# SyncE's loads in written order through the mixing of a diffusion trunk, with shared decay buffers and later closings

## The chip, the cores and the metric

The kernel runs on one core of one Trainium2 chip. Its time is the device time of one execution in microseconds; the median over three executions is given. The core's engines are TensorE (PE, with its weight loads as PEld), VectorE (DVE), ScalarE (ACT), GpSimd (POOL) and SyncE (SP). SyncE computes nothing: its queue issues nearly all loads and many stores. Each engine works through its own queue in order, and waits on semaphores for the others.

## The reference

One layer of a diffusion trunk over 1024 latent tokens and 256 context tokens, width 1024, in float32. It has a half-step SwiGLU feed-forward, then the mixing, then a second half-step feed-forward, each modulated by a condition vector. The mixing projects the normalised tokens by one matrix into four retention heads (key and value width 128) and four gated linear attention heads, called GLA below (key width 64, value width 128, with a low-rank gate). Cut to its core:

```python
x = x + 0.5 * m_l[2] * swiglu(modulate(rms_norm(x, norm1_w), m_l[0], m_l[1]), ffn1_w1, ffn1_w3, ffn1_w2)
...  # the same for ctx; then, on both normalised and modulated:
p_lat, p_ctx = jnp.split(h_lat @ w_in, IN_SPLITS, axis=-1), jnp.split(h_ctx @ w_in, IN_SPLITS, axis=-1)

# retention, one step of the scan over chunks of 128 tokens
scores = jnp.einsum('bhid,bhjd->bhij', qc, kc) * decay
o = jnp.einsum('bhij,bhje->bhie', scores, vc) + jnp.einsum('bhid,bhde->bhie', qc * q_dec, s)
s = chunk_dec * s + jnp.einsum('bhjd,bhje->bhde', kc * k_dec, vc)

# GLA, one step of the scan over chunks of 64 tokens, g the log gates
b = jnp.cumsum(gc, axis=-2)
rel = jnp.exp(jnp.where(tri[:, :, None], b[:, :, :, None, :] - b[:, :, None, :, :], -jnp.inf))
scores = jnp.einsum('bhid,bhjd,bhijd->bhij', qc, kc, rel)
o = jnp.einsum('bhij,bhje->bhie', scores, vc) + jnp.einsum('bhid,bhde->bhie', qc * jnp.exp(b), s)
s = jnp.exp(b_last[:, :, 0, :])[..., None] * s + jnp.einsum('bhjd,bhje->bhde', kc * jnp.exp(b_last - b), vc)

# closing
r = merge_heads((o_ret - mu) * lax.rsqrt(var + EPS)) * ret_norm_w * jax.nn.silu(p[3])
gl = merge_heads(o_gla * lax.rsqrt(mean(o_gla * o_gla) + EPS)) * gla_norm_w * jax.nn.silu(p[7])
y = jnp.concatenate([r, gl], axis=-1) @ w_out
x = x + m_l[5] * y
x = x + 0.5 * m_l[8] * swiglu(modulate(rms_norm(x, norm3_w), m_l[6], m_l[7]), ffn2_w1, ffn2_w3, ffn2_w2)
return rms_norm(x, final_norm_w)
```

Both scans run in both directions. The scans over the latent tokens start from the final states of the scans over the context. Every head's output is normalised over its 128 channels (GLA by the root mean square, retention by mean and variance), multiplied by a weight and a gate, and projected back by `w_out`.

## The kernel before

A product in float32 is made of three matmuls with the operands split into a high and a low part (`whi`, `wlo` of the weights, `hh`, `hl` of the activations): ScalarE copies the high part (line 62), VectorE subtracts it (line 63). A weight goes through a ring of six `raw` buffers, loaded by SyncE (line 273), and is then split. Activations lie as 128 channels by 512 tokens, in two halves of the latent tokens, `tg` 0 and 1; context tokens are 256 columns wide, and for the value projections a weight tile is 288 wide, 256 values and 32 gate columns.

The program runs in phases: the first feed-forward, the context's projections (`ctx_proj`, whose results go to memory as `cgk`, `crk`, `cgv`, `crv`, line 1112 for the last), the mixing's set-up (`mix_setup`: position tables, `wg`, `p89Tc`), the mixing itself (`lat_phase`), the output projection (`mixed_in` and `mixed_out`), the second feed-forward.

In `lat_phase` a small planner writes the program. Its filling is the list of large projections of the latent tokens (`lat_units`; a unit such as `gv0` is one projection of a few heads). Beside it run four lanes, written as generators: the context's final states, the gates, the four GLA heads and the four retention heads. The planner holds a clock of TensorE's time (`self.now`) and guesses of when VectorE, ScalarE and GpSimd come free (`self.clk`, moved by `self.w`). A lane yields the time at which its next step has its operands; the planner emits that step once its time has come, and otherwise the next piece of a projection.

TensorE takes the instructions in the order in which they were written (`pe_order`). On the other engines a scheduler with priorities sets the order: it may put a load or a copy far ahead of its place in the program. Weight loads have a raised priority (line 300 and what calls it).

A head's output of one half ends in a chain that is called its closing. GLA: square the output and sum it, take the power −1/2 on GpSimd (`pow_half`, line 1168), scale by it on ScalarE (line 1375, tile `t`). Retention: statistics (lines 1489 and 1491), power on GpSimd, scale on VectorE (line 1500, tile `t2r`). Then `finish`: four transposes on TensorE (line 1150), a multiply by the norm's weight, and by the gate where its tile is ready (such a block is "gated"), and a store to `mixd` in memory. `mixed_in` loads the blocks back (line 1672), multiplies by the gate those that lack it, and splits them.

`decays` makes three decay tables per retention head by exponentials on ScalarE (line 1200), combines them on VectorE and stores them to `decd`. The GLA heads build their within-chunk products in levels: tiles `AB` (lines 1262, 1276) are scaled on VectorE, copied to `zq` and `zk` (lines 1265 to 1267), and multiplied on TensorE (lines 1285 and 1320).

Of the kernel before, what the change touches and what calls it, by code (L numbers as in the profile page):

```python
# [10 lines left out]
F32 = mybir.dt.float32  # L11
# [5 lines left out]
P = 128  # L17
# [13 lines left out]
class Trunk:  # L31
# [834 lines left out]

    def pe_order(self):
        return self.tc.manual_schedule(engines={mybir.EngineType.PE})

# [276 lines left out]
    def finish(self, on, tg, wcol, hb, pool):  # L1146
        nc = self.nc
        pt = self.psB()
        for c in range(4):
            nc.tensor.transpose(pt[:, c * P:(c + 1) * P], on[:, c * P:(c + 1) * P], self.ident)  # L1150
        mx = self.t2(pool)
        if hb in self.gated:
            sg = self.tile(pool, [P, 512], F32, "sg", 2)
            nc.sync.dma_start(sg, self.sgd[hb * P:(hb + 1) * P, tg * 512:(tg + 1) * 512])
            nc.vector.scalar_tensor_tensor(out=mx, in0=pt, scalar=wcol, in1=sg, op0=ALU.mult, op1=ALU.mult)
            self.w("v", 0.75)
        else:
            self.late.add((hb, tg))
            nc.scalar.activation(mx, pt, AF.Copy, scale=wcol)
            self.w("a", 0.62)  # L1160
        self.w("p", 0.6)
        self.store.dma_start(self.mixd[hb * P:(hb + 1) * P, tg * 512:(tg + 1) * 512], mx)
# [7 lines left out]
    def gate_lane(self, pool):  # L1170
# [18 lines left out]
        for h in range(4):  # L1189
            yield max(self.clk["a"], self.now + 5 * (h > 0)), 0, ()  # L1190
            self.decays(h, pool)
            self.done[f"D{h}"] = self.w("p", 0.6, self.w("v", 0.6, self.w("a", 1.6)))

    def decays(self, h, pool):
        nc = self.nc
        tab = lambda i: self.tab[:, i * P:(i + 1) * P]
        dec, u = self.tile(pool, [P, 3, P], F32, "dec", 1), self.t2(pool)[:, :P]
        lf, lb = self.lg[:, h:h + 1], self.lg[:, 4 + h:5 + h]
# [4 lines left out]
        nc.vector.tensor_tensor(out=dec[:, 0, :], in0=dec[:, 0, :], in1=u, op=ALU.add)  # L1203
        self.store.dma_start(self.decd[h], dec.rearrange("p i t -> p (i t)"))

# [26 lines left out]
    def gla_lane(self, h, pool):  # L1232
# [126 lines left out]
        for tg in LATTG:  # L1359
# [10 lines left out]
            r = self.tile(pool, [P, 4], F32, "rr", 4)  # L1370
            self.pow_half(r, ss, 1.0 / P)
            on = self.t2(pool)
            for c in range(4):
                s = slice(c * P, (c + 1) * P)
                nc.scalar.activation(on[:, s], po[:, s], AF.Copy, scale=r[:, c:c + 1])
            t = self.w("v", 0.2, self.w("v", 0.7, self.w("a", 0.62)))
            ons.append((self.w("a", 1.15, self.w("p", 1.3, t)), on))
        for tg in LATTG:
            yield ons[tg][0], 0.9, ()
            self.finish(ons[tg][1], tg, self.col("gla_norm_w")[:, h:h + 1], 4 + h, pool)  # L1380

    def ret_lane(self, h, pool):
# [95 lines left out]
        for tg in LATTG:  # L1478
# [14 lines left out]
            self.pow_half(r, mv[:, :, 1], 1.0)  # L1493
            t = self.w("p", 1.3, self.w("v", 1.4))
            if tg == 0:
                ready, sc, qf = decay(1, ps)
            on = t2()
            for c in range(4):
                s = slice(c * P, (c + 1) * P)
                nc.vector.tensor_scalar(out=on[:, s], in0=po[:, s], scalar1=mv[:, c, 0:1], scalar2=r[:, c:c + 1],  # L1500
                                        op0=ALU.subtract, op1=ALU.mult)
            ons.append((self.w("v", 1.5, t), on))
        for tg in LATTG:
            yield ons[tg][0], 0.9, ()
            self.finish(ons[tg][1], tg, self.col("ret_norm_w")[:, h:h + 1], h, pool)
# [120 lines left out]
    def lat_phase(self, pool):  # L1626
# [17 lines left out]
        lanes = [[g, 0, 0, ()] for g in lanes]  # L1644
        with self.pe_order():
            for lane in list(lanes):
# [107 lines left out]
    def run(self):  # L1754
# [243 lines left out]
        def feed2():  # L1998
# [42 lines left out]
UNITS = ("gv0", "gk0", "gq0", "rk0", "rq0", "rv0", "rk1", "rq1", "gk1", "gq1", "gv1", "gg0", "rk2", "rq2", "rv1", "rg0", "gg1",  # L2041
         "rk3", "rq3", "rg1", "gg2", "rg2", "gg3", "rg3")
LAG = 0.7
WAHEAD, WLIVE = 3, 5
# [98 lines left out]
```

## Time and profile before

| | us |
|---|---|
| runs | 2121.08, 2123.88, 2125.47 |
| median | 2123.88 |
| the profiled execution's own time | 2122.97 |
| its span, first to last instruction | 2121.1 |
| TensorE busy | 2097.8 |
| VectorE, ScalarE, GpSimd busy | 1522.5, 961.3, 176.9 |
| last matmul of the context's projections starts | 913.14 |
| first matmul of the mixing's projections starts | 913.26 |

In a timeline row stand: start, duration, engine, line, operation, output <- inputs, shapes, count; in brackets the engine's idle time before it and what ended it. A row of waits names the waiting instruction, what released it, the total, the count and the longest. In a row of windows stand: the stretch and its length; the busy time of TensorE, its weight loads, VectorE, ScalarE and GpSimd, each with its number of instructions; the granted TensorE clock as a share of full speed; the share of the DMA engines; GB/s. A queue is marked by a q (SPq is SyncE's).

### The profile page before, as it was taken

How to read it: one execution, taken by the hardware profiler on the slowest of the kernel's cores; microseconds unless marked ns; L12 is line 12 of the kernel's file. 1: busy time of each engine (PE TensorE's matmuls, PEld its weight loads, DVE VectorE, ACT ScalarE, POOL GpSimd, SP SyncE). 2: the span in 40 equal slices, each digit the busy share in tenths (PEclk: the TensorE clock that was granted, in tenths of full speed). 3: DMA queues.
4: the chain of work that ended last, by engine and by line, in shares of the span. 5: the costliest groups of instructions: out<-in, count | busy, mean ns of one | idle time of the engine just before them, and what ended most of it. 6: DMA issues, size and time to landing. Idle time of an engine off the chain costs nothing.

```text
span 2121.1 us, 32909 instructions
## 1 busy us (share of the span) xinstructions
PE 2097.8 (99%) x11558; PEld 1807.9 (85%) x11558; DVE 1522.5 (72%) x2810; ACT 961.3 (45%) x1786; POOL 176.9 (8%) x294
## 2 busy tenths in 40 slices
PE   8999999999999999999999999999999999999998
PEld 7888888888889999987889988888888888888888
DVE  7889999766677765857675565567866676666676
ACT  4433434345545555667442443344433434344552
POOL 0101111110000000011010000100011110111000
PEclk9999999999999999999999999999999999999999
DMA  9266867569886654476462445452244443466773
GB/s 339 85 219 234 281 218 257 185 203 338 277 290 206 205 180 159 142 239 224 140 194 95 162 141 178 158 208 75 90 140 154 158 167 136 148 243 234 237 241 124
DMA packets 214726, 408.50 MB, mean 193 GB/s; under 512 B 26208, under 2 KB 52256, under 8 KB 214560
## 3 DMA queue, kind: packets, MB, share of 16 engines
q1 hardware_dynamic: 185456, 330.24, 47.5%
q0 software_dynamic: 18848, 61.87, 7.3%
q10 hardware_dynamic: 10256, 14.29, 1.8%
q8 instruction: 90, 1.47, 0.3%
q14 instruction: 76, 0.62, 0.1%
HBM read 320.04 MB, written 86.26 MB: 192 GB/s over the span
## 4 chain that ended last, share of the span: by engine, by line
PE 47%; issue 3%; DVE 1%; POOL 1%; ACT 0%; POOLq 0%; DVEq 0%; ACTq 0%
PE psa L67 9%; PE psa L69 8%; PE psa L68 8%; PE psb L69 5%; PE psb L68 5%; PE psb L67 5%; PE psa L1574 3%; PE psb L1285 1%; PE psb L1441 1%; POOL rr L1168 0%; PE psb L1485 0%; PE psb L1459 0%; PE psb L1349 0%; PE psb L1150 0%; PE psb L1365 0%
## 5 line engine op out<-in xcount | busy, mean ns | idle before, releaser
L62 ACT ACTIVATE whi<-raw 128x512 fp32r<-128x512 f32 (+1 forms) x471 | 292.7, 624 | 564.0 <-PE psa L68 182.5
L67 PE MATMUL psa<-hh,whi 128*128 128x512 f32 (+1 forms) x1444 | 531.8, 368 | 0.2 <-ACT s L332 0.2
L69 PE MATMUL psa<-hh,wlo 128*128 128x512 f32 (+1 forms) x1444 | 525.7, 364 | 0.0
L68 PE MATMUL psa<-hl,whi 128*128 128x512 f32 (+1 forms) x1444 | 525.6, 364 | 0.0
L63 DVE TENSOR_TENSOR wlo<-raw,whi 128x512 fp32r<-128x512 f32 (+1 forms) x471 | 318.5, 679 | 226.2 <-ACT whi L62 222.6
L67 PEld LDWEIGHTS psa<-hh,whi 128*128 128x128 f32 x1444 | 273.2, 189 | 47.0 <-issue 5.3
L69 PEld LDWEIGHTS psa<-hh,wlo 128*128 128x128 f32 x1444 | 272.8, 189 | 43.4
L68 PEld LDWEIGHTS psa<-hl,whi 128*128 128x128 f32 x1444 | 273.1, 189 | 40.8 <-DVE hl L63 0.3
L67 PE MATMUL psb<-hh,whi 128*128 128x512 f32 (+1 forms) x680 | 259.6, 382 | 0.0
L69 PE MATMUL psb<-hh,wlo 128*128 128x512 f32 (+1 forms) x680 | 259.4, 382 | 0.0
L68 PE MATMUL psb<-hl,whi 128*128 128x512 f32 (+1 forms) x680 | 259.4, 382 | 0.0
L68 PEld LDWEIGHTS psb<-hl,whi 128*128 128x128 f32 x680 | 127.8, 188 | 24.8
L69 PEld LDWEIGHTS psb<-hh,wlo 128*128 128x128 f32 x680 | 127.8, 188 | 24.7
L67 PEld LDWEIGHTS psb<-hh,whi 128*128 128x128 f32 x680 | 127.8, 188 | 24.6
L285 ACT ACTIVATE whi<-s 128x512 fp32r<-128x512 f32 (+1 forms) x164 | 101.0, 620 | 87.0 <-PE psa L68 38.0
L290 DVE TENSOR_TENSOR wlo<-s,whi 128x512 fp32r<-128x512 f32 (+1 forms) x164 | 106.9, 675 | 29.6 <-ACT whi L285 29.4
L373 POOL DMA_DIRECT2D gd<-s x154 | 83.7, 543 | 370.5 <-DVE s L364 285.1
L130 DVE CUSTOM_DVE_ANT_0 junk<-ada,condc,cols 128x1024 bf16<-128x1024 f32 x62 | 79.2, 1278 | 5.9 <-DMA ada<-in_adaT 3.8
L1168 POOL TENSOR_TENSOR nr<-nr,mhalf 128x4 f32<-128x4 f32 (+1 forms) x11 | 10.9, 992 | 687.3 <-DVE nr L1167 445.5
L372 DVE TENSOR_TENSOR s<-s,s 128x512 f32<-128x512 f32 x88 | 59.0, 684 | 0.5
L359 ACT ACTIVATE s<-s 128x512 f32<-128x512 f32 x57 | 36.0, 632 | 47.8 <-DVE s L336 47.7
L1574 PE MATMUL psa<-whi,hh 128*128 128x256 f32 x192 | 56.1, 292 | 0.0
(428 smaller groups left out, 3941.4 us busy)
## 6 DMA issues: line engine op xcount, KB each, us to landing
raw<-in_w SPq DMA_DIRECT2D x242, 256.0 KB, 3.4
s<-in_w SPq DMA_DIRECT2D x198, 256.0 KB, 4.1
gd<-s POOLq DMA_DIRECT2D x154, 256.0 KB, 2.9
ada<-in_adaT SPq DMA_DIRECT2D x76, 512.0 KB, 4.6
hh<-gd SPq DMA_DIRECT2D x58, 256.0 KB, 4.1
hl<-gd SPq DMA_DIRECT2D x58, 256.0 KB, 4.1
sd<-s POOLq DMA_DIRECT2D x44, 256.0 KB, 3.1
raw<-sd SPq DMA_DIRECT2D x44, 256.0 KB, 2.8
```

Source lines behind the costliest of these rows:

```text
L62: nc.scalar.activation(hi, src, AF.Copy)
L63: (eng or nc.vector).tensor_tensor(out=lo, in0=src, in1=hi.bitcast(F32), op=ALU.subtract)
L67: mm(ps, wa[0], xa[0], start=start, stop=False, skip_group_check=more)
L68: mm(ps, wa[0], xa[1], start=False, stop=False, skip_group_check=more)
L69: mm(ps, wa[1], xa[0], start=False, stop=stop, skip_group_check=more)
L130: nc.vector.tensor_tensor_reduce(out=self.junk, in0=t, in1=self.cs[s], scale=1.0, scalar=self.col("ada_b")[:, j:j + 1], op0=ALU.mult, op1= ...
L285: self.nc.scalar.activation(hi[:, :n], src, AF.Copy)
L290: self.nc.vector.tensor_tensor(out=lo, in0=src, in1=hi.bitcast(F32), op=ALU.subtract)
L359: self.nc.scalar.activation(o, t, AF.Silu)
L372: sub = lambda o, a, b: nc.vector.tensor_tensor(out=o, in0=a, in1=b, op=ALU.subtract)
L373: put = lambda i, t: self.store.dma_start(self.gd[i, f // 2], t)
L1574: mm(o, x[p], y[q], start=k == 0 and n == 0 and c % 2 == 0, stop=k == KD - 1 and n == 2, skip_group_check=True)
```

## The change

The diff, whole but for two lines that set a constant's place:

```diff
-    def pe_order(self):
-        return self.tc.manual_schedule(engines={mybir.EngineType.PE})
+    def pe_order(self, *more):
+        return self.tc.manual_schedule(engines={mybir.EngineType.PE, *more})
@@ finish
         if hb in self.gated:
-            sg = self.tile(pool, [P, 512], F32, "sg", 2)
+            sg = self.t2(pool)
             nc.sync.dma_start(sg, self.sgd[hb * P:(hb + 1) * P, tg * 512:(tg + 1) * 512])
@@ gate_lane
         for h in range(4):
-            yield max(self.clk["a"], self.now + 5 * (h > 0)), 0, ()
+            yield max(self.clk["a"], self.now + DECAT * (h > 0)), 0, ()
             self.decays(h, pool)
@@ decays
-        dec, u = self.tile(pool, [P, 3, P], F32, "dec", 1), self.t2(pool)[:, :P]
+        t, u = self.t2(pool)[:, :3 * P], self.t2(pool)[:, :P]
+        dec = t.rearrange("p (i t) -> p i t", i=3)
...
-        self.store.dma_start(self.decd[h], dec.rearrange("p i t -> p (i t)"))
+        self.store.dma_start(self.decd[h], t)
@@ gla_lane
             self.pow_half(r, ss, 1.0 / P)
+            yield self.w("p", 1.3, self.w("v", 0.9, self.w("a", 0.62))), 0, ()
             on = self.t2(pool)
             for c in range(4):
                 s = slice(c * P, (c + 1) * P)
                 nc.scalar.activation(on[:, s], po[:, s], AF.Copy, scale=r[:, c:c + 1])
-            t = self.w("v", 0.2, self.w("v", 0.7, self.w("a", 0.62)))
-            ons.append((self.w("a", 1.15, self.w("p", 1.3, t)), on))
+            ons.append((self.w("a", 1.15), on))
         for tg in LATTG:
-            yield ons[tg][0], 0.9, ()
+            yield ons[tg][0] + FIN, 0.9, ()
@@ ret_lane
-            t = self.w("p", 1.3, self.w("v", 1.4))
+            t = self.w("p", 1.3, self.w("v", 1.45))
             if tg == 0:
                 ready, sc, qf = decay(1, ps)
+            yield t, 0, ()
             on = t2()
...
-            ons.append((self.w("v", 1.5, t), on))
+            ons.append((self.w("v", 1.4), on))
         for tg in LATTG:
-            yield ons[tg][0], 0.9, ()
+            yield ons[tg][0] + FIN, 0.9, ()
@@ lat_phase
-        with self.pe_order():
+        with self.pe_order(mybir.EngineType.SP):
@@ constants
+DECAT = 12
+FIN = 2
```

It has four parts. Inside the mixing SyncE's queue, too, keeps the order in which the planner writes it. The decay tables lie in the ring of six shared `t2` buffers in place of a single buffer of their own, and the heads' tables are 12 us apart in the plan where they were 5 apart; the gate tiles of `finish` lie in the same ring. In the closings the scaling becomes a step of its own, which the planner emits at the time at which it expects GpSimd's power. The closing transposes stand 2 us later in the plan.

The instructions stay nearly the same: 10748 on TensorE in both, 2812 on VectorE (two multiplies of `mixed_in` become two in `finish`), two copies fewer on ScalarE, 1293 on SyncE. From the mixing on a line number of the profile is one or two higher in the changed kernel (1276 becomes 1277, 1500 becomes 1502).

The rows below are those of the engines' queues. First SyncE's queue before the change, in the middle of the context's projections (`raw` is a weight's buffer, `in_wgv0` the first projection of the mixing, `in_w12` a weight of the feed-forward):

```order
L273 DMA raw_1994_9066<-in_w12 128x512
L273 DMA raw_2173_9817<-in_wgv0 128x288
L273 DMA raw_2180_9827<-in_wgv0 128x288
L273 DMA raw_2183_9833<-in_wgv0 128x288
L273 DMA raw_2186_9839<-in_wgv0 128x288
L273 DMA raw_2189_9857<-in_wgv0 128x288
L273 DMA raw_2192_9875<-in_wgv0 128x288
L1091 DMA cgk<-s_2028_9169 128x256
```

The same weight, `raw_2173`, in SyncE's queue of the changed kernel, 57 places further on, at the start of the mixing:

```order
L1112 DMA crv<-s_2145_9744 128x256
L929 DMA wg_2150_9762<-in_wgb 16x4x64
L928 DMA wg_2150_9762<-in_wgf 16x4x64
L929 DMA wg_2150_9762<-in_wgb 16x4x64
L932 DMA p89Tc_2151_9768<-p89d 32x256
L939 DMA t2_2152_9774<-in_lvlmask 128x128
L939 DMA t2_2154_9778<-in_lvlmask 128x128
L939 DMA t2_2156_9782<-in_lvlmask 128x128
L939 DMA t2_2158_9786<-in_lvlmask 128x128
L1021 DMA t2_2170_9812<-crk 128x256
L1022 DMA t2_2171_9813<-crv 128x2x128
L273 DMA raw_2173_9817<-in_wgv0 128x288
```

The first weight loads of the mixing moved from ahead of the context's stores to behind the last of them, the tables, the masks and two loads of the context's results. On TensorE nothing moved here: the first matmul on the high part of this weight follows the last matmul of the context's projections in both. On ScalarE the table load and the exponential `kd` (line 915) stand ahead of the copy of line 1111 that this `crv` store saves; before, they stood behind it.

Second, VectorE's queue in the second GLA and retention heads, before (`bst` and `bmv` are a retention closing's statistics, `rr` what GpSimd raises to its power, `AB0` and `AB1` the GLA head's tiles):

```order
L1489 BN_STATS bst_2629_12359<-psb_2628_12346 128x6 x4
L1491 BN_AGGR bmv_2630_12360<-bst_2629_12359 128x2 x4
L1167 TENSOR_SCALAR rr_2631_12369<-bmv_2630_12360 128x4
L1276 TENSOR_TENSOR AB0_2537_11781<-AB0_2537_11781,L_2536_11778 128x2x8x32
L1500 TENSOR_SCALAR t2r_2632_12372<-psb_2628_12346,bmv_2630_12360,rr_2631_12369 128x128 x4
L1276 TENSOR_TENSOR AB1_2540_11790<-AB1_2540_11790,L_2539_11787 128x2x8x32
```

and in the changed kernel:

```order
L1490 BN_STATS bst_2632_12413<-psb_2631_12400 128x6 x4
L1492 BN_AGGR bmv_2633_12414<-bst_2632_12413 128x2 x4
L1167 TENSOR_SCALAR rr_2634_12423<-bmv_2633_12414 128x4
L1277 TENSOR_TENSOR AB0_2565_11891<-AB0_2565_11891,L_2564_11888 128x2x8x32
L1277 TENSOR_TENSOR AB1_2568_11900<-AB1_2568_11900,L_2567_11897 128x2x8x32
L1502 TENSOR_SCALAR t2r_2636_12486<-psb_2631_12400,bmv_2633_12414,rr_2634_12423 128x128 x4
```

The scaling of the retention output moved behind the second `AB`.

Third, TensorE's queue at the last closing but one, near the end of the mixing, in the changed kernel (`psa` with `hh0`, `hl0` are the last projections, `t2_2966` is GLA's scaled output):

```order
L69 MATMUL psa_2972_14630<-hh05_2007_9096,wlo_2957_14527 128x512
L1150 MATMUL psb_2974_14654<-ident_4_82,t2_2966_14600 128x128 x4
L67 MATMUL psa_2972_14630<-hh06_2009_9098,whi_2956_14526 128x512
```

This closing, of the last GLA head and the first half, stands 30 matmuls of projections ahead of the output projection; the last one of all, for the second half, stands 12 ahead of it. Before, the last closing was a retention head's, with 90 matmuls of projections behind it. That GLA head's two closings are gated in the changed kernel and were not before.

## The prediction

> **What bounds the kernel now.** I read the page's busy table and the core's clock first, then TensorE's waits in the stretch that the change touches, then for each of them what its releaser had waited for, and last SyncE's timeline where the stretch begins.
>
> ```profile
> PE 2097.8 (99%) x11558; PEld 1807.9 (85%) x11558; DVE 1522.5 (72%) x2810; ACT 961.3 (45%) x1786; POOL 176.9 (8%) x294
> core 0: 2121.1 us, clock 0.995
> ```
>
> TensorE is busy for 99% of the span, at nearly its full clock. The change neither adds nor removes a matmul (10748 instructions stand on TensorE in both). So there are only three ways to move the time: TensorE's idle time, its clock, and the order in which matmuls of different shapes follow each other. The first question is how much idle time the mixing has to give.
>
> ```profile
> PE psb L1285 <- DVE zk L1266: 1.8, 1, 1.8
> PE psb L1150 <- DVE t2r L1500: 1.6, 1, 1.6
> PE psb L1320 <- DVE AB L1276: 1.2, 1, 1.2
> PE psb L1459 <- ACT t L1159: 0.8, 1, 0.8
> PE psb L1441 <- DVE Sr L1448: 0.4, 1, 0.4
> ```
>
> These are all of TensorE's waits from 930 to 1420 us, by line and releaser (us in total, times, the longest): 1.8 + 1.6 + 1.2 + 0.8 + 0.4 = 5.8 us. The first one costs more than its idle time. The windows behind it show the granted clock (PEclk, the third figure from the end):
>
> ```profile
> 1012.00:1013.00 1.00, 0.54 (x5) 0.57 (x5) 1.00 (x4) 0.13 (x1) 0.00 (x0) 0.98 0.77 240
> 1013.00:1014.00 1.00, 1.00 (x7) 1.00 (x6) 1.00 (x4) 0.00 (x0) 0.04 (x1) 0.50 0.09 35
> 1016.00:1017.00 1.00, 1.00 (x9) 1.00 (x9) 1.00 (x3) 0.95 (x4) 0.00 (x0) 0.82 0.00 0
> ```
>
> After 1.8 us of idling the clock stood at half from about 1013.0 to 1016.4. That is 3.4 us in which half the work was lost, 1.7 us. So at most 5.8 + 1.7 = 7.5 us can be won in the mixing.
>
> **The waits that the change goes after.** Each has its cause one step further back:
>
> ```profile
> ACT dec L1200 <- DMA decd<-dec: 2.1, 1, 2.1
> DVE t2r L1500 <- POOL rr L1168: 1.0, 1, 1.0
> 1142.83 1.36 DVE L1500 TENSOR_SCALAR t2r<-psb,bmv,rr 128x128 f32<-128x128 f32 x4 [0.93 <-POOL rr L1168]
> 1144.11 1.28 DVE L1276 TENSOR_TENSOR AB<-AB,L 128x512 f32<-128x512 f32 x2
> ```
>
> The single `dec` buffer held ScalarE for 2.1 us until its store had read it; `zk` stands behind it, and TensorE's 1.8 us behind that. With the table in one of six shared buffers and the heads 12 us apart this wait has no cause left. In the second and third stall VectorE stood in front of GpSimd's power: 1.0 and 0.93 us. At 1142.83 VectorE idled 0.93 and scaled for 1.36 before the `AB` that TensorE missed by 1.2. In the changed order that `AB` stands ahead of the scaling, as the rows in the section on the change show, so VectorE comes to it 0.93 + 1.36 = 2.3 us earlier, more than 1.2. In the second and the fourth stall the late work is the scaling or the copy of a closing itself; there the closing is put 2 us later in the written order. The edit removes no work: two multiplies move on VectorE and two copies leave ScalarE, both with idle time in the mixing, and they are worth nothing to TensorE. What is late next is unknown: the lanes now run in another order from their second head on, so small stalls of the same kind can fall elsewhere. Bounds: 0, and the 5.8 us that the old order had. I take 2, about two of the smaller ones. Gain: (5.8 − 2) + 1.7 = 5.5 us.
>
> Matmuls of 128 columns between those of 512 have a price too:
>
> ```profile
> 1357.83 0.39 PE L69 MATMUL psa<-hh,wlo 128*128 128x512 f32 x1
> 1358.06 0.60 PE L1150 MATMUL psb<-ident,t2r 128*128 128x128 f32 x4
> 1358.41 0.48 PE L67 MATMUL psa<-hh,whi 128*128 128x512 f32 x1
> 1358.73 0.39 PE L68 MATMUL psa<-hl,whi 128*128 128x512 f32 x1
> ```
>
> The first matmul after a switch takes 0.32 to the next start, the one before the transposes 0.23, so a switch costs about 0.09. I count 80 switches back to large matmuls in the mixing before and 84 after: +0.4 us.
>
> **The queue of loads.** This term decides. Before, the scheduler moved the first six weight loads of the mixing some 50 us ahead; in the change SyncE's queue keeps the written order, and the first weight stands behind everything that was written before it. What stands there has these issue times before (SyncE's timeline; weight loads that stood between them are left out):
>
> ```profile
> 861.46 0.33 SPq L273 DMA_DIRECT2D raw<-in_wgv  x1
> ...
> 914.18 0.38 SPq L1112 DMA_DIRECT2D crv<-s  x1
> ...
> 915.66 0.39 SPq L1112 DMA_DIRECT2D crv<-s  x1
> 916.14 0.70 SPq L928 DMA_DIRECT2D wg<-in_wgf  x1
> ...
> 918.90 0.58 SPq L928 DMA_DIRECT2D wg<-in_wgf  x1
> 919.53 0.59 SPq L929 DMA_DIRECT2D wg<-in_wgb  x1
> 920.17 0.58 SPq L932 DMA_DIRECT2D p89Tc<-p89d  x1
> 920.80 1.36 SPq L939 DMA_DIRECT2D t<-in_lvlmask  x3
> ...
> 923.16 0.42 SPq L1021 DMA_DIRECT2D t<-crk  x1
> 923.63 0.43 SPq L1022 DMA_DIRECT2D t<-crv  x1
> ```
>
> The last `crv` store is the gate: it saves what ScalarE copies out of the last context matmul, so it can't be issued before that copy. In ScalarE's changed order a table load and one small exponential stand ahead of it.
>
> ```profile
> 913.14 0.28 PE L69 MATMUL psa<-whi,hl 128*128 128x256 f32 x1
> 913.26 0.30 PE L67 MATMUL psa<-whi,hh 128*128 128x288 f32 x1
> 913.10 0.37 ACT L1111 COPY s<-psa 128x256 f32<-128x256 f32 x1 [0.38 <-PE psa L69]
> 914.25 1.28 ACT L915 ACT_TABLE_LOAD   x1
> 915.54 0.22 ACT L915 ACTIVATE kd<-s 128x16 f32<-128x16 f32 x1
> raw<-in_wgv SPq DMA_DIRECT2D x10, 144.0 KB, 2.8
> DMA to landing us min/median/max: 2.0/3.5/7.1
> L62 ACT ACTIVATE whi<-raw x19: 428/445/632, 908.4 to 934.2; 128x288 fp32r<-128x288 f32 x16, 128x512 fp32r<-128x512 f32 x3
> ```
>
> Worked forward: the first copy ends at 913.47; table load 1.28 and exponential 0.22 bring 914.97; the second copy 0.37 brings 915.3, and the last `crv` store is issued then and done at 915.7. (The two rows ahead of the last are the landing of weights from 905 to 935 us, in us from issue.) Behind the store come three `wg` loads at a pitch of 0.63 (917.6), `p89Tc` at 0.63 (918.2), four masks at 0.46 (920.1), `crk` and `crv` at 0.47 (921.0). Only now is the first weight issued. It lands 2.8 later (923.8) and ScalarE's split takes 0.45 (924.3). TensorE stands in order: its next matmul after the last context matmul is the one on this weight, in both kernels, and started at 913.26 with no gap. So TensorE idles from 913.3 to 924.3: **+11.0 us**. The later weights follow each other every 0.4 us at the queue and nothing more is lost on them. Bounds: with eleven issues at the shortest row of this view, 0.33, and the fastest landing of a weight in this window, 2.0, it is 915.3 + 0.33·11 + 2.0 + 0.45 = 921.4, a gap of 8.1; with the median landing of all weights here, 3.5, 11.7.
>
> After such a gap the clock will drop as it did at 1013. One window of 3.4 us at half speed costs 1.7 us, and I take that. The start of the span bounds it:
>
> ```profile
> 20.00:25.00 5.00, 4.55 (x15) 3.65 (x16) 4.96 (x11) 2.22 (x6) 0.00 (x0) 0.50 1.00 376
> 25.00:30.00 5.00, 4.09 (x24) 3.50 (x22) 1.89 (x4) 1.55 (x5) 0.00 (x0) 0.84 1.02 381
> ```
>
> There the clock stayed at half for at least 5 + 1.6 = 6.6 us, about twice as long, which would cost 3.4. The other end is 0: the half-speed time may run out inside the gap. [...]
>
> **The end of the mixing.** The last closing transposes now come 30 large matmuls (30 at 0.23, 6.8 us) before the output projection for the half that it begins with; before, the last ones of all stood at 1358.06, 20 us before it. What hangs on them is a store and a load through memory:
>
> ```profile
> L1162 POOL DMA_DIRECT2D mixd<-t x16: 539/597/606, 1082.9 to 1359.8; - x16
> DMA to landing us min/median/max: 2.3/3.2/5.2
> ```
>
> Transposes 0.6, the multiply about 0.7, store 3.2, load about 3, and a split 0.6: 8.1 us. The block is the eighth of eight, used some 3.4 us into the projection, so 6.8 + 0.4 + 3.4 = 10.6 us are there, and I add nothing. If both landings took the 5.2 of the row, it would cost 1.7 us.
>
> **Sum**, against the profiled execution's own time of 2122.97 us (span 2121.1): 2122.97 − 5.5 + 0.4 + 11.0 + 1.7 = 2130.6. That execution lies 0.9 below the median of the runs shown, 2123.88, and these span 4.4 us, so I forecast 2131.
>
> **Rivals.**
>
> *The early weights are not missed, and the kernel is faster.* The mechanism is the removal of the five stalls alone. It decides if the first weight is issued by about 916, at which point gap and clock cost only the 5 us that the stalls give back; issued by 910 there is no gap. For it: SyncE's queue holds little else there, and no row shows that it must be as slow as before. Against it: the last `crv` store can't be issued before 915, and eleven issues stand between. With no gap: 2122.97 − 5.5 + 0.4 = 2117.9. Chance 0.09.
>
> *The gap is at its short end and all stalls go.* 2122.97 + 8.1 + 0.9 (half a window's price) − 7.5 + 0.4 = 2124.9, up to 2128. For it: the DMA engines are less loaded when the early loads are gone. Against it: it needs every term at its favourable end. Chance 0.18.
>
> *The change does not do what it says*: for every stall taken away another of its size comes, since GpSimd's power has the same length and the planner only guesses it. 2122.97 + 0.4 + 11.0 + 1.7 = 2136.1; a second window at half clock or a tail of that size lands in the same place. For it: the planner's own guess put the old stalls where they are. Against it: the `dec` buffer and the `AB` row have measured room. Chance 0.18.
>
> *My forecast*, a slower kernel at about 2131 (2128 to 2134): 0.55.
>
> **How the numbers follow.** About 0.2%, 4.2 us, is what can be told from no change here: faster means under 2119.6, slower over 2128.1. Faster 0.09 is the first rival. The second rival lies within, 0.18. Slower is the forecast and the third, 0.73. The range leaves out the first rival and the end of the third: 2121 to 2138.
>
> **What would show it.** A wait of about 11 us of TensorE on ScalarE's `whi` (line 62) or its load at 913 us, the first `raw<-in_wgv` issued near 921 rather than 861, PEclk of 0.5 just after, and the whole mixing some 11 us late from there. No wait of ScalarE on `decd`; no wait of the scaling on GpSimd ahead of `AB`. I am wrong if TensorE runs through 913 without a gap, or if the waits of the mixing behind 930 still add up to 5 us.

## The result and the profile after

The changed kernel takes 2141.27 us (median of six runs, 2139.0 to 2145.72), the kernel before 2122.91 on the same chip (six runs, 2121.08 to 2125.5): 18.4 us more, ratio 1.0088 with a 95% interval of 1.0078 to 1.0099. The profiled execution took 2144.64 us, at the upper end of the runs, with a span of 2142.6.

The page and the cores' view, after:

```profile
PE 2104.7 (98%) x11558; PEld 1811.5 (85%) x11558; DVE 1525.7 (71%) x2810; ACT 962.5 (45%) x1784; POOL 175.4 (8%) x294
core 0: 2142.6 us, clock 0.991
```

TensorE's busy time grew by 6.9 us although its instructions are the same, and its mean clock fell from 0.995 to 0.991. So there is lost time in two forms, as idle time and as matmuls at half clock. TensorE's waits from 905 to 1450 us, after:

```profile
PE psa L67 <- ACT whi L62: 10.7, 1, 10.7
PE psb L1006 <- DVE t L1001: 5.0, 2, 3.8
PE psb L1286 <- ACT zq L1266: 3.8, 2, 2.0
PE psb L1442 <- DVE Sr L1449: 0.3, 1, 0.3
```

The first is the gap at the start of the mixing. Of the five stalls of before, four are gone; only the 0.3 on L1442 has its counterpart in the 0.4 on L1441. Two new kinds stand there: the transposes of the context's GLA states (L1006) wait 5.0 us in two places, and the first product of each of two GLA heads (L1286) waits 3.8 us in all, for `zq`. (L1286 is the line that was L1285; the 1.8 us of before stood there at a later product of the first head, for `zk`.) Behind the gap that is 9.1 us, where before had 5.8.

The queue and TensorE at the gap, after (timelines of SyncE, then of TensorE):

```profile
916.77 0.33 SPq L1112 DMA_DIRECT2D crv<-s  x1
...
921.63 0.38 SPq L1021 DMA_DIRECT2D t<-crk  x1
922.05 0.43 SPq L1022 DMA_DIRECT2D t<-crv  x1
922.53 13.64 SPq L273 DMA_DIRECT2D raw<-in_wgv  x16
```

```profile
914.63 0.28 PE L69 MATMUL psa<-whi,hl 128*128 128x256 f32 x1
925.62 0.61 PE L67 MATMUL psa<-whi,hh 128*128 128x288 f32 x1 [10.71 <-ACT whi L62]
```

The last `crv` store goes out at 916.77, the first weight at 922.53, and TensorE's first matmul on it starts at 925.62. In this execution the context's matmuls ended 1.5 us later than in that of before (914.63 against 913.14), so 1.5 us of the difference of the two profiles lie ahead of the mixing. The clock behind the gap and behind the longest of the new stalls (windows, after):

```profile
917.00:919.00 2.00, 0.00 (x0) 0.00 (x0) 0.00 (x0) 0.00 (x0) 0.80 (x2) 0.62 0.30 93
919.00:925.00 6.00, 0.00 (x0) 0.00 (x0) 1.47 (x4) 0.00 (x0) 4.07 (x9) 0.50 0.53 151
925.00:931.00 6.00, 5.38 (x21) 5.17 (x22) 3.01 (x7) 2.95 (x7) 0.00 (x0) 0.50 0.81 230
931.00:933.00 2.00, 2.00 (x17) 2.00 (x16) 0.46 (x1) 0.44 (x1) 0.00 (x0) 0.96 0.44 120
1056.00:1060.00 4.00, 4.00 (x12) 3.13 (x11) 0.88 (x3) 1.26 (x5) 1.08 (x2) 0.50 0.88 276
1060.00:1062.00 2.00, 2.00 (x13) 1.76 (x12) 0.00 (x0) 0.60 (x1) 0.00 (x0) 0.79 0.33 97
```

In the window from 917 to 919 the mean of 0.62 puts the drop to half at about 917.5, inside the gap; the clock stayed there until about 931.2, so 5.5 us of matmuls ran at half speed: 2.75 us lost. Behind the stall that ended at 1055.5 it stayed at half until about 1060.8, 2.65 us lost, and behind the first stall of 2.0 us another 1.7 (the clock is 0.77, 0.50 and 0.88 in the three windows of 2 us from 1012 on). The sum for the two profiled executions: 10.7 of gap, 2.75 of clock behind it, 9.1 − 5.8 = 3.3 of stalls, 2.65 + 1.7 − 1.7 = 2.65 of clock behind stalls, 1.5 ahead of the mixing: 20.9 of the measured 2144.64 − 2122.97 = 21.7.

### The profile page after: what moved, and what is told of

It is laid out like the page before. It is cut to its first block, busy times and chain, and to the rows that moved or that the text cites. A ratio compares the mean times of both kernels' runs of the same rounds, so it can differ in the third digit from the quotient of the medians.

```text
span 2142.6 us, 32855 instructions
## 1 busy us (share of the span) xinstructions
PE 2104.7 (98%) x11558; PEld 1811.5 (85%) x11558; DVE 1525.7 (71%) x2810; ACT 962.5 (45%) x1784; POOL 175.4 (8%) x294
## 4 chain that ended last, share of the span: by engine, by line
PE 87%; issue 4%; DVE 4%; DMA 3%; ACT 1%; SPq 0%; POOL 0%; ACTq 0%; DVEq 0%; POOLq 0%
PE psa L67 16%; PE psa L68 16%; PE psa L69 16%; PE psb L67 9%; PE psb L69 9%; PE psb L68 9%; PE psa L1576 3%; PE psb L626 3%; PE psb L1286 2%; DVE junk L130 1%; PE psb L1486 1%; PE psb L1442 1%; DVE wlo L63 0%; DMA ada<-in_adaN 0%; DMA Sr<-s0r 0%
## 5 line engine op out<-in xcount | busy, mean ns | idle before, releaser
L1511 ACT ACTIVATE pv<-psa 128x512 f32<-128x512 f32 x50 | 29.6, 592 | 72.4 <-PE psa L69 51.4
```

## The experiments

Two theories stood at the beginning. **A**: SyncE's order costs the start alone, and the four stalls are the new plan's. **B**: SyncE's order makes the stalls too, because loads stand in line behind loads that wait. All times are medians, ratios are against the kernel before on the same chip. No run leaves out any work of the reference.

| run | time, us | ratio and its 95% interval |
|---|---|---|
| the change | 2141.3 | 1.0088, 1.0078 to 1.0099 |
| 1: without SyncE's order | 2120.2 | 0.9986, 0.9977 to 0.9994 |
| 2: SyncE's order alone | 2149.0 | 1.0124, 1.0110 to 1.0138 |
| 3: six weights early | 2134.0 | 1.0050, 1.0037 to 1.0062 |
| 4: decay tables alone | 2122.9 | 0.9996, 0.9987 to 1.0005 |
| 5: closings alone | 2118.4 | 0.9981, 0.9972 to 0.9990 |
| 6: AB first | 2148.4 | 1.0121, 1.0107 to 1.0135 |
| 7: start rewritten, AB first | 2136.5 | 1.0071, 1.0058 to 1.0085 |
| 8: as 1, AB first | 2119.8 | 0.9987, 0.9979 to 0.9996 |
| 9: as 5, FIN 0 | 2122.0 | 0.9994, 0.9985 to 1.0003 |
| 10: start rewritten | 2132.2 | 1.0042, 1.0029 to 1.0056 |
| 11: as 10, two decay buffers | 2131.4 | 1.0035, 1.0022 to 1.0048 |
| 12: as 1, tables 5 us apart | 2117.6 | 0.9974, 0.9964 to 0.9983 |
| 13: as 10, DONE 10 | 2134.3 | 1.0058, 1.0046 to 1.0071 |
| 14: as 1, DONE 10 | 2137.4 | 1.0075, 1.0061 to 1.0089 |
| 15: as 10, weights written earlier | 2129.4 | 1.0034, 1.0021 to 1.0046 |
| 16: as 12, AB first | 2118.1 | 0.9978, 0.9969 to 0.9987 |

### 1 and 2: SyncE's order taken away, and alone

```diff
# 1, against the change
-        with self.pe_order(mybir.EngineType.SP):
+        with self.pe_order():
# 2, against the kernel before, with pe_order as in the change
-        with self.pe_order():
+        with self.pe_order(mybir.EngineType.SP):
```

> The changed kernel with SyncE's queue in the mixing left to the scheduler again; all else of the change stays. In the changed kernel TensorE idles 10.7 us at 914 us with the clock at half for 5.5 us of work behind it (2.7 us lost), and 9.1 us in four stalls between 1010 and 1140 us. Theory A (the gap is SyncE's order, the four stalls are the new plan's): 2141.3 - 10.7 - 2.7 = 2127.9, the four stalls still there. Theory B (SyncE's order makes the stalls too, by loads that stand in line behind waiting ones): no gap and no more than 2 us of stalls, about 2117.

> The kernel before with SyncE's queue in written order in the mixing, and nothing else of the change. Theory A: gap and half clock alone, 2122.9 + 10.7 + 2.7 = 2136.3, and the old stalls of 5.8 us where they were. Theory B: about 2141, with stalls of some 9 us at new places.

Without it the change runs at 2120.2, alone it runs at 2149.0. So SyncE's order costs 2141.3 − 2120.2 = 21 us in the change and 26 us by itself, while all the rest of the change together gains some 3 us. Neither theory had as much as 26: run 2 was expected at 2136.3 or about 2141. TensorE's waits in run 1 (905 to 1420 us):

```profile
PE psb L1286 <- DVE zk L1267: 2.7, 1, 2.7
PE psb L1006 <- DVE t L1001: 0.8, 1, 0.8
PE psb L1026 <- DMA t<-crk: 0.7, 1, 0.7
PE psb L1442 <- DVE t L979: 0.7, 1, 0.7
```

The gap is gone, and the stalls on `zq` with it; those on L1006 shrank from 5.0 to 0.8. Theory A, 2127.9, falls: 21 us are far more than the 13.4 of the start. Theory B's 2117, with no more than 2 us of stalls, is 3 us too low: they still add up to 4.9 us, and the largest, 2.7 us, is not SyncE's order's. Run 2 shows the mechanism in its plainest form. First TensorE, then the waits of ScalarE and of SyncE that belong to it, then SyncE's timeline, all of run 2:

```profile
1054.19 0.80 PE L67 MATMUL psa<-hh,whi 128*128 128x512 f32 x1 [6.98 <-ACT whi L62]
ACT whi L62 <- DMA raw<-in_wrk: 5.7, 1, 5.7
SPq L1387 <- DMA decd<-dec: 15.5, 1, 15.5
1014.05 0.47 SPq L273 DMA_DIRECT2D raw<-in_wrv  x1
1030.20 0.33 SPq L1387 DMA_DIRECT2D dec<-decd  x1
...
1048.01 1.80 SPq L1400 DMA_DIRECT2D rs<-rqd  x4
1049.85 0.90 SPq L273 DMA_DIRECT2D raw<-in_wrk  x2
```

From 1014.5 SyncE stands 15.5 us on one load of a decay table. It waits for the single buffer `dec`, out of which the tables of the heads are still being stored (the last such store is issued at 1027.9). Behind it come a head's rope loads, with waits of their own, and only then the next weight, at 1049.85. ScalarE splits it at 1053.5, and TensorE idled for 7.0 us. A weight needs nothing that the table has. In the kernel before these loads waited too, 10.4 us in two waits, and TensorE's list has no wait on a weight there: the scheduler had put the weights that it needed next ahead of them (SyncE's waits from 940 to 1300 us, before):

```profile
SPq L1387 <- DMA decd<-dec: 10.4, 2, 5.6
```

### 3: the first six weights written early

```diff
# against the change, at the start of lat_phase; the first six load_half take these
+        with self.tc.high_priority(offset=WPRI):
+            self.first = [self.raw_half(self.I["wgv0"][k]) for k in range(6)]
```

> The changed kernel with the first six weight loads of the mixing written ahead of the part that SyncE takes in written order, so that the scheduler puts them early again (50 us ahead in the queue, as in the kernel before). The seventh still stands behind the context's loads. If the place of the first loads is the cause of the gap: TensorE starts the mixing at 913 to 914 us, uses six weights of 12 matmuls in 9.5 us, and waits about 2.7 us for the seventh, issued at 922.5; 10.7 + 2.7 shrink to 2.7 or, with a clock drop, 4.4: 2141.3 - 9 to 10.7 = 2130.6 to 2132.3. If ScalarE's order (table load ahead of the last copy) is the cause: no change, 2141.

Measured 2134.0, against 2130.6 to 2132.3 expected. TensorE starts the mixing without a gap and waits for the seventh weight instead:

```profile
924.30 0.61 PE L67 MATMUL psa<-whi,hh 128*128 128x288 f32 x1 [3.07 <-ACT whi L62]
```

3.1 us against 2.7 worked out ahead. That the place of the first loads in the line made the gap is shown.

### 4, 5 and 9: the parts of the plan alone

```diff
# 4, against the kernel before
-        dec, u = self.tile(pool, [P, 3, P], F32, "dec", 1), self.t2(pool)[:, :P]
+        t, u = self.t2(pool)[:, :3 * P], self.t2(pool)[:, :P]
+        dec = t.rearrange("p (i t) -> p i t", i=3)
-            yield max(self.clk["a"], self.now + 5 * (h > 0)), 0, ()
+            yield max(self.clk["a"], self.now + 12 * (h > 0)), 0, ()
# 5, against the kernel before: the hunks of the change in gla_lane, ret_lane and finish, FIN = 2
# 9: as 5, with
-FIN = 2
+FIN = 0
```

> The kernel before with only the decay tables in the shared buffers and the heads 12 us apart. If the single buffer is the whole cause of the first stall (1.8 us and 1.7 us by the clock): 2122.9 - 3.5 = 2119.4. If another wait of ScalarE or VectorE is right behind it: 2122 to 2124, with a stall of 1 to 2 us at the same matmuls. If the shared ring of six buffers is too small for it, a wait on a t2 buffer appears and the time is over 2125.

> The kernel before with the closings' part of the change alone: the scaling as a step of its own, FIN, the gate tiles in the shared ring; the decay table in its own single buffer, heads 5 us apart, SyncE left to the scheduler. The whole change without SyncE's order ran at 2120.2 (before 2123.7 on the same chip), and the decay part alone at 2122.9. Theory A (the gain of 3.5 is the closings'): 2120 to 2121, the three stalls on L1150, L1320 and L1459 (1.6, 1.2 and 0.8 us) gone, the stall of 1.8 on L1285 kept with its clock drop. Theory B (the gain needs both parts): 2122 to 2124.

> The closings' part alone (which ran at 2118.4, 4.0 under the kernel before on its chip) with FIN at 0: the scaling as a step of its own and the gate tiles in the shared ring stay, the closing transposes stand in the plan where they stood. If the step is the gain: 2118 to 2119.5, the stalls on L1150, L1320 and L1459 gone. If FIN is: 2121 to 2123, with a stall of 1 us or more on L1150.

The decay tables alone change nothing (0.9996, 0.9987 to 1.0005). The wait on the single buffer went, and the stall stayed and grew. Run 4, first TensorE, then the waits of ScalarE and VectorE ahead of it:

```profile
PE psb L1286 <- DVE zk L1267: 2.2, 1, 2.2
ACT t L999 <- DVE cT L997: 3.9, 1, 3.9
DVE qk L1403 <- DMA rq<-rqd: 1.6, 1, 1.6
```

VectorE stands 1.6 us on a rope load that has not landed, the context's gates behind it come late, ScalarE waits 3.9 us for them, and `zk` is late behind both. That the rope load makes the stall is read from this chain and not shown; run 12 speaks for part of it at most. In the kernel before VectorE came to that product at 1002.99 without a wait, because a split and two steps of the decay table stood ahead of it; these stand elsewhere now. The closings alone run at 2118.4, 4.0 us under the kernel before on its chip and below both forecasts, and this is TensorE's whole list from 930 to 1420 us in run 5:

```profile
PE psb L1285 <- DVE zk L1266: 1.5, 1, 1.5
PE psb L1441 <- DVE Sr L1448: 0.4, 1, 0.4
```

The three stalls of 1.6, 1.2 and 0.8 us are gone. With FIN at 0 they are gone too; the old one at `zk` stands with 1.3 us, a new one of 1.1 us comes at `zq`, and the time is 2122.0. So the step, with the gate tiles in the shared ring, made the three stalls go. Its time alone is not told from that of the kernel before (0.9985 to 1.0003). The intervals of 5 and 9 overlap by a little, so that FIN is worth some 2 us is likely and not shown; run 9 was forecast at 2118 to 2119.5, or at 2121 to 2123 with a stall on L1150, and is neither as a whole.

### 6 and 8: AB written ahead of the gates' reloads

```diff
# 6 against the change, 8 against run 1: these lines of gla_lane moved behind the loads of AB and vg
         for tg in LATTG:
-            g[tg], L[tg] = self.tile(pool, [P, 512], F32, "sc", 2), self.tile(pool, [P, 512], F32, "L", 2)
-            nc.sync.dma_start(g[tg], self.ggd[h, tg])
-            nc.sync.dma_start(L[tg][:, :508], self.gLd[h, tg][:, :508])
```

> The changed kernel with eight loads of a GLA head (AB and vg, whose data and buffers are ready) written ahead of its four reloads of gates (sc and L), which wait for their buffers. In the changed kernel SyncE stands 17.3 us on the first sc reload and 5.2 on the L reloads, and AB is issued only at 1004.6 us; TensorE then idles 2.0 us at 1010 us and 1.8 us at 1124 us on zq, which is copied from AB. If that line behind a waiting load is the cause: both stalls on zq gone, 3.8 us and 1.7 us of clock: 2141.3 - 4 to 5.5 = 2136 to 2137.5; the gap of 10.7 at 914 unchanged. If the stall is the plan's: 2141, same stalls. The weights behind the sc reload stay as late as they are, so the stall of 3.8 us at 1052 us stays in both.

> The whole change without SyncE's order (2120.2), and AB written ahead of the gates' reloads. With the scheduler free to choose, written order should matter little: 2119 to 2121. If it moves the loads of AB earlier and frees SyncE for the retention heads' loads, the stall of 2.7 us on zk at 1011 us shrinks: 2116 to 2118.

Run 6 went the other way: 2148.4, 7 us more than the change. My theory of that one stall fell. `AB` of the first head was issued from 980.8 instead of 1004.6 us, and the stall only moved from 1012 to 1025 us, to `zk`, because the gates' reload still comes when it comes; and in the second head, where `AB` is what waits, the gates now stand behind it, and VectorE waits 6.0 us for their `sc`:

```profile
1025.49 1.13 PE L1287 MATMUL psb<-zq,zk 128*128 128x128 f32 x8 [3.04 <-DVE zk L1268]
1124.27 2.08 PE L1287 MATMUL psb<-zq,zk 128*128 128x128 f32 x8 [5.93 <-ACT zq L1267]
```

Run 8, the same text with the scheduler free, is at 2119.8, no different from run 1. So in written order a swap of two groups of loads cost 7 us here and 4 us on top of run 10 (run 7, below), and with the scheduler none.

### 7, 10 and 11: the start written in another order, and two decay buffers

```diff
# 10, against the change (7 has run 6's edit as well)
-        self.masks(pool)
+        with self.tc.high_priority(offset=WPRI):
+            self.first = [self.raw_half(self.I["wgv0"][k]) for k in range(6)]
...
+            for _ in range(5):
+                self.now += next(fill)[2]
+            self.masks(pool)
             for lane in list(lanes):
                 step(lane)
# 11, against 10; three small statistics buffers go from two to one, not shown
-        dec = self.tile(pool, [P, 3, P], F32, "dec", 1)
+        dec = self.tile(pool, [P, 3, P], F32, "dec", 2)
```

> SyncE still in written order, but the order written differently: the first six weights ahead of the ordered part, the masks and the context's loads behind the eighth weight, and AB ahead of the gates' reloads. If the place of the loads in the line is the whole cost of SyncE's order, this comes back to the time without it: no gap at 914, at most 5 us of stalls, 2120 to 2124. If written order costs something by itself (weights can't pass a load that waits, whatever the order), stalls of over 5 us remain behind 1040 us: 2126 to 2130.

> The changed kernel with only the start of the mixing written in another order: the first six weights ahead of the ordered part, masks and the context's loads behind the eighth weight. The order of AB and of the gates' reloads is that of the change. In the changed kernel the gap of 10.7 us and 5.5 us at half clock behind it cost 13.4. If these are all that the start costs: 2141.3 - 13.4 = 2127.9, and the rest over the kernel without SyncE's order (2120.2), 7.7 us, lies in stalls behind 1000 us. If the late start also hid something (the lanes had more time before TensorE came): 2130 to 2134, with larger stalls behind 1000 us.

> As the run with the start written differently, with two buffers in place of one for the decay table that a retention head loads back (three small statistics buffers of VectorE go from two to one to make room, and only VectorE uses them). In the changed kernel SyncE stands 16.6 us on the load of the second head's table, which waits for the first head's use, with that head's ropes and the second GLA head's AB and gates behind it. If that line makes the stalls on zq near 1112 to 1126 us: 2 to 4 us less than the run beside it, and no wait of over 5 us on that load. If the loads behind it wait for their own buffers anyway (rope has one, rq and rs two): no difference, and SyncE stands on L1396 or L1399 instead.

Run 10 is at 2132.2: the start is worth 9.1 us, not 13.4, and 12.0 us are left over run 1. Part of the missing 4 us is seen at the place itself: 1.6 us of waits on the copies of the first unit (`p`, lines 1552 and 1555), where the change had none. Run 7, with run 6's edit on top, is at 2136.5, above run 10 as run 6 is above the change, and above both of its forecasts. So no order that I wrote brings the time back to that of the scheduler. What SyncE waits for from 940 to 1300 us shows the difference. The largest rows of run 1 first, then of run 10:

```profile
SPq L273 <- DVE wlo L63: 88.5, 22, 10.8
SPq L273 <- DVE Sr L1449: 23.1, 3, 11.7
SPq L1399 <- DMA rkd<-pv: 15.9, 3, 7.2
```

```profile
SPq L1242 <- PE psb L1366: 44.8, 4, 19.7
SPq L1242 <- DVE sc L1330: 41.2, 2, 28.5
SPq L1413 <- DMA rvd<-pv: 26.4, 3, 17.3
SPq L1388 <- DVE t2r L1470: 18.7, 1, 18.7
```

With the scheduler free, SyncE's longest wait by far is that of weights (line 273) that stand at the head of the queue for a free buffer, 88.5 us: they are as early as the six buffers let them. In run 10 that wait is 6.3 us. In written order SyncE spends its waits on the lanes' loads (gates, line 1242; values, line 1413; decay table, line 1388), and what stands behind these comes when they have gone, lane loads and weights alike. The lane loads can be seen directly ahead of the stalls on `zq`: ScalarE waits for `AB` there (waits of ScalarE from 1005 to 1013 us, then from 1112 to 1127 us, after), and the first of these loads stood behind a reload of the gates that waited 17.3 us.

```profile
ACT zq L1260 <- DMA AB<-gqd: 2.1, 1, 2.1
ACT zq L1260 <- DMA AB<-gqd: 5.0, 1, 5.0
```

The weights come in a burst. In the change five weights were issued from 1039.7 to 1044.8 us, behind a head's rope loads, and this is what stands on VectorE ahead of the late context's gates (timeline, after; the splits `wlo` with the steps of the gates between them):

```profile
1047.30 0.67 DVE L63 TENSOR_TENSOR wlo<-raw,whi 128x512 fp32r<-128x512 f32 x1
...
1049.10 0.43 DVE L980 TENSOR_TENSOR t<-t,t 128x256 f32<-128x256 f32 x1 [0.48 <-ACT t L877]
1049.63 0.69 DVE L63 TENSOR_TENSOR wlo<-raw,whi 128x512 fp32r<-128x512 f32 x1
1050.71 0.69 DVE L63 TENSOR_TENSOR wlo<-raw,whi 128x512 fp32r<-128x512 f32 x1 [0.39 <-ACT whi L62]
...
1051.84 0.68 DVE L63 TENSOR_TENSOR wlo<-raw,whi 128x512 fp32r<-128x512 f32 x1
...
1052.83 0.66 DVE L63 TENSOR_TENSOR wlo<-raw,whi 128x512 fp32r<-128x512 f32 x1
...
1055.05 0.42 DVE L1001 TENSOR_TENSOR t<-t,t 128x256 f32<-128x256 f32 x1
1055.53 0.69 PE L1006 MATMUL psb<-ident,t 128*128 128x128 f32 x2 [3.82 <-DVE t L1001]
```

The burst is not all of it. The load of the context's keys to which this stall goes back (line 991) stood behind the same rope loads (SyncE's timelines, after, then run 1):

```profile
1040.26 1.12 SPq L991 DMA_DIRECT2D t<-cgk  x2
1016.28 1.10 SPq L991 DMA_DIRECT2D t<-cgk  x2
```

In the change TensorE is ready for the transposes 11.5 us behind this issue and waits 3.8; in run 1 it comes 23.7 us behind it and does not wait. The lead alone does not decide either: in run 2 TensorE comes 10.2 us behind it and does not wait.

Run 11 tests one link of the line. The wait of 18.7 us on the decay table is gone, and the time is the same (2131.4; the intervals overlap): SyncE stands on the next load instead, the queries of line 1399, 21.8 us. That was the rival's forecast, but the row names another reason than the rope's buffers: the store of the projected queries (`rqd`). The single buffer of the table is not the cause.

### 12 and 16: a version that beats both

```diff
# 12, against run 1; 16 has run 8's edit as well
-DECAT = 12
+DECAT = 5
```

> The whole change without SyncE's order (2120.2), with the decay tables 5 us apart in the plan as before (DECAT 5), still in shared buffers. The closings alone ran at 2118.4 with the table's old buffer and a stall of 1.5 us on zk at 1011 us; with the shared buffers and 12 us the stall was 2.7, because VectorE stood on a rope load that had not landed. If the 12 us are what puts VectorE in front of that load: 2117 to 2118.5, stall on zk under 1.5. If the shared ring is: 2120, the stall of 2.7 us stays.

> The fastest so far (the whole change without SyncE's order and with the decay tables 5 us apart: 2117.6, ratio 0.9974) with AB written ahead of the gates' reloads. The remaining stalls are 1.2 us on zq at 1011 us and 0.4 on L1442. With the scheduler free: 2117 to 2119; if the earlier AB removes the 1.2: 2116.

Run 12 is the fastest, 2117.6, ratio 0.9974 (0.9964 to 0.9983): the whole change without SyncE's order and with the tables at their old distance. From 905 to 1420 us TensorE has two waits left, 1.2 us on L1286 and 0.4 on L1442. VectorE still stands 1.6 us on the rope load, against 2.4 in run 1, so my reason for the 2.7 us of run 1, that the 12 us put VectorE in front of that load, is wrong, or a part of it at most. What makes the stall behind it shorter I have not traced. Its distance to run 5 is within their intervals. Run 16, with `AB` first, is no different.

### 13, 14 and 15: what the rest of SyncE's order is

```diff
# 13 against run 10, 14 against run 1
-DONE = 6
+DONE = 10
# 15, against run 10
-WAHEAD, WLIVE = 3, 5
+WAHEAD, WLIVE = 5, 6
```

> As the run with the start written differently (2132.2), with DONE at 10 in place of 6: a lane's loads are written 4 us later behind the projection whose stored result they read. SyncE's order stays. If the stalls behind 1000 us come from loads in the line that wait for data not yet stored (rqd, rvd) and hold the weights behind them, SyncE's waits on these shrink and the stalls on L1006 (4.6 us) and zq (4.4 us) with them: 2126 to 2129. If the line is late whatever the plan's margin: 2131 to 2134.

> The control for it: the whole change without SyncE's order (2120.2), with DONE at 10. If the margin matters only to a queue in written order, 2119 to 2122. If it helps or hurts the plan by itself, the difference shows here.

> As the run with the start written differently (2132.2), with each weight load written up to two places of its unit earlier (WAHEAD 5, WLIVE 6), so that two more weights stand ahead of a retention head's and a GLA head's loads in SyncE's line. Theory: what the order costs behind 1000 us is that weights wait behind lane loads and then come in bursts, whose splits stand in ScalarE's and VectorE's queues ahead of the context's gates (L1006) and of zq. Then the stall of 3.5 us on L1006 shrinks to about 1 and the time to 2127 to 2130. Rival: the late lane loads themselves (AB, the gates) make the stalls; then 2131 to 2135, with stalls on L1006 and zq as before.

With the lanes' loads written 4 us later (DONE is the plan's margin behind the projection whose result they read), run 13 is at 2134.3, no gain over run 10. Only the control makes it readable: without SyncE's order the same margin costs 17 us (2137.4, where 2119 to 2122 was expected), because the last heads then come too late: TensorE waits 4.1 us on L1442, 3.6 us for a closing and 5.2 us for the output projection's input. So with DONE at 10 SyncE's order costs nothing more, 2134.3 against 2137.4, where with DONE at 6 it cost 12. And the waits that it made are gone from run 13: L1006 has 0.2 us, `zq` none (L1286 still has 1.3, for another operand); in their place stand the end's 3.6 and 3.3 us, which the control has too. This speaks for lane loads that wait for data not yet stored as the head of the line. Two terms of a plan that shifts as a whole can't be parted further by this pair, so I call it likely, not shown.

Run 15, weights two places earlier in the line, is at 2129.4, 2.8 us under run 10, with intervals that overlap; the stalls on L1006 go from 4.6 to 3.9 us and those on `zq` from 4.4 to 3.0. The direction is that of the theory of late weights, the size is a fraction: I had expected about 1 on the longest and it is 2.8. TensorE comes to these transposes 11.4 us behind the context's load here, as late as in the change. So the burst may be part of it. The lane loads' own lateness is the likelier larger part, and what it makes of the 12 us exactly stays open.

## Why the prediction failed where it did

**The start was right.** A wait of TensorE on `whi` of 10.7 us, against 11.0; the first weight issued at 922.5, against 921.0, of which 1.5 are the context's later end. Run 3 shows the cause. Taken away, the start gave back 9.1 us (run 10) and not the 13.4 that the profile put there.

**The clock behind it was under-sized.** The prediction took 1.7 us, the price of half clock as long as the 3.4 us behind the stall at 1013 us in the kernel before; 2.75 were lost, within its bounds of 0 and 3.4. Half clock lasted to 5.5 us behind the restart (from 925.62 to about 931.2), longer than those 3.4 us and shorter than the 6.6 or more at the start of the span. The drop came at about 917.5, 2.6 us behind the last context matmul (914.63 + 0.28), and the clock was still at half when TensorE restarted at 925.62 (0.50 in the windows from 919 to 925 and from 925 to 931). So the half-speed time did not run out inside the gap, and the bound of 0 was not reached. What sets how long it lasts, no run shows.

**The step that failed** is the sentence "What is late next is unknown … I take 2". It bounded the new stalls by 0 and the 5.8 us of the old ones, as if only the plan could make them. SyncE's order was charged for the start, and put at nothing behind it without a reason. ("Nothing more is lost" on the later weights held: TensorE has no second wait on `whi`.) The runs show 21 us for SyncE's order, and 12 of them are left when the start is mended. In the change that is 9.1 us of stalls and 4.35 us of clock behind them, instead of 2 and 0: the prediction's own sign of being wrong, waits of 5 us behind 930. The check that was missing is the one that the prediction made at the start and nowhere else: to walk along the new queue and ask of each load what it waits for and what stands behind it. The profile of before had a row for it: SyncE waited 10.4 us on the decay table's loads, and a weight behind it in written order would have shared the wait.

**The first stall of before was misread.** "This wait has no cause left" holds for the wait on the buffer, not for TensorE's stall: run 4 has it at 2.2 us without that wait. A rope load that VectorE stands on is in its chain there; in the kernel before the table's own steps had stood on VectorE while that load landed. How much of the stall is that load's, no run shows.

**The closings were right**: the stalls on L1150, L1320 and L1459 are gone in runs 1 and 5. The gain of 5.5 us without SyncE's order was put a little high: run 1 gained 3.5 and run 5 4.0, medians against medians. That these gains are those of the stalls is not quite shown, since run 9 lost the same three, got one new one of 1.1 us, and gained 0.9, within the noise.

**The end of the mixing was right**: no stall there in the change. The 0.4 us for four more switches between shapes were not measured by themselves.

**The rivals.** "The change does not do what it says", at 2136.1, came nearest in time, and not by its mechanism: the old stalls did go, and no wait on GpSimd's power stands ahead of the new ones. The range ended at 2138, because all the terms behind the start together were given no more than the 5.8 us that the old order had had.

## What to carry to other kernels

SyncE's queue in written order handed the wait of one load on to those behind it: in run 2 a weight stood behind a wait of 15.5 us, and TensorE idled 7.0 us for that weight. Before such an order is given to the queue that brings the weights, go through it load by load: what does it wait for (a buffer, a store, an engine), how long does the trace say, and which load behind it has nothing to do with that. And when a wait is removed, look at the same place for what lands or ends next within its length, and for what the removed work had been standing in front of, before its time is booked as a gain.

## What the runs showed of the hardware that was not expected

The price of a stall varied, since a clock drop followed some stalls and not others. In run 7 a stall of 2.8 us at 1013.8 was followed by half clock and one of 2.65 us at 1041.9 by none (windows of run 7):

```profile
1014.00:1016.00 2.00, 2.00 (x10) 2.00 (x11) 1.97 (x5) 0.14 (x1) 0.54 (x1) 0.50 0.13 37
1042.00:1044.00 2.00, 2.00 (x10) 1.69 (x11) 1.45 (x6) 1.97 (x7) 0.54 (x1) 1.00 0.75 197
```

In run 3 even one of 3.1 us, at 1044.6, was followed by none. Of the stalls in the mixing that these profiles show, none under 1.7 us was followed by a drop; the shortest that was had 1.79 (run 15). Five executions of run 10 took 2127.9, 2131.6, 2132.2, 2132.8 and 2136.9 us at mean clocks of 0.996, 0.995, 0.995, 0.994 and 0.993: 9 us between executions of one program, and the time goes with the clock. So one profiled execution of run 10 tells a sum to some 5 us, no better. That longer stalls make a wider spread the runs do not show: run 12, with hardly a stall, spread over 4.5 us in ten executions, and run 6, with more than the change, over 1.7 in four.
